# Covariance attention on one Trainium2 core: half of one unit's store leaves as 68 and 60 partitions in place of 85, 32 and 11

## The chip, the core and the metric

The kernel runs on one core of a Trainium2 chip. The time is that of the device, in microseconds (us). Of the kernel before there are three runs: 129.61, 129.66 and 130.15, median 129.66. A profiled execution comes beside them, 129.72, and all durations in this document are from its trace. The core has compute engines (PE for matmuls, DVE, ACT and POOL for the rest), a queue engine (SP) that issues most of the transfers here, and 16 DMA engines that carry them.

## The reference

Q, K and V are `[8, 12, 512, 64]` in float32. For each of the 96 heads the columns of Q and K are normalised over the 512 positions, a 64 x 64 matrix is made from them, and its softmax multiplies V:

```
Q_norm = Q / (norm(Q, axis=-2) + 1e-10)
K_norm = K / (norm(K, axis=-2) + 1e-10)
attn = softmax(einsum('bhnd,bhne->bhde', Q_norm, K_norm), axis=-1)
out = einsum('bhnd,bhde->bhne', V, attn)
```

There is much to move for little to compute: 37.75 MB are read and 12.58 MB written.

## The kernel before, in words

The 96 heads are worked on in S = 12 units of 8 heads, numbered 0 to 11. Each unit has 1 MB of Q, 1 MB of K, 1 MB of V and 1 MB of output. Two units make a pair that shares its tiles of V (there are W = 6 pairs).

For one unit, Q and K are loaded (`load_qk`, L219 and L221), cast to bf16 (`cast_qk`), squared (`square`) and multiplied to Gram matrices (`grams`, L260). The sums of squares give the norms (`sums`, `fold`, `norms`, `powers`). The scaled matrix goes through the softmax (`scale_k`, `logits`, `scales_q`, `exps`, `normalise`). V is loaded (`load_v`, L225), cast and transposed, and the product with it is made in four parts (`outs`, L338), each of which `ocopy` (L205 on ACT, L207 on DVE) copies into the unit's output tile `so`: 128 partitions, each with two halves (r = 0 and 1) of 1024 numbers, that is 4096 bytes a half. The pool of `so` has 6 buffers.

The order of all instructions on every engine comes from a planner (`Order`): it is given each piece of work with an estimated cost, what must come before it and a rank, and it lists the pieces in the order in which it would begin them. The store of a unit is one piece for it, whose cost doesn't depend on how the store is cut.

All loads but the two pieces of the first K are issued from the SP queue, and so are all stores, in the planner's order. `store(s, i)` (L227 to L236) issues one transfer for a unit (L234), 1024 KB, with one exception. Unit S - SPLIT = 9, the third from the end, is stored half by half, and each half is cut along its partitions as the table `CUTS` says (L228 to L232): half 0 as partitions 0 to 85, 85 to 117 and 117 to 128, and half 1 whole. Behind these four transfers come those of unit 10 and unit 11, and then the kernel waits until all stores have landed; the profile shows that wait under L512.

In DRAM the 128 partitions of one half are 128 rows of 4096 bytes that lie one behind the other, so each partition of a half is one packet of 4096 bytes for one DMA engine.

Of the kernel before, what the change touches and what calls it, by code (L numbers as in the profile page):

```python
# [56 lines left out]
 'V_PACE': 0.7666,  # L57
 'ST_LAG': 6.0835,
 'SPLIT': 3,
 'CUTS': (((0, 85), (85, 117), (117, 128)), ((0, 128),))}  # L60

D = 64
T = 32
# [453 lines left out]
```

## Time and profile before

| what | value |
|---|---|
| median of three runs | 129.66 us (129.61 to 130.15) |
| profiled execution, its own time | 129.72 us |
| its span, first to last instruction | 127.6 us |
| busy share of PE, DVE, ACT, POOL | 63%, 63%, 67%, 37% |
| DMA packets, bytes | 11601, 50.59 MB |
| share of the 16 DMA engines' span for SP's queue (q1) | 94.2% |
| instruction blocks of 16 KB (q8) | 14, 0.6% |
| last compute instruction ends | 114.9 us |
| issue of the four transfers of unit 9 | from 109.94 us on |
| issue of unit 10 and unit 11 | 112.69 and 114.89 us |

The span is cut into 40 equal slices in the page, about 3.2 us each; a digit is the busy share of a slice in tenths. In the list of DMA issues, KB is the size of one transfer, and the last number is the time from its issue to its landing. A landing is known from the completion marks: each DMA engine that has a part of a transfer sends one mark behind its last packet. A wait table names the waiting engine and line, what it waited for, the total, the number of times and the longest wait.

### The profile page before, as it was taken

Reading aid. Unit: us, or ns where it says so; the run is one execution under the profiler, and the core shown is the slowest. Engines: PE = TensorE matmul, PEld = TensorE weight load, DVE = VectorE, ACT = ScalarE, POOL = GpSimd, SP = SyncE. Lnnn points to the kernel's source line nnn. Section 1 sums busy time; section 2 is a strip of 40 time slices with the busy share of each in tenths; the row PEclk is TensorE's granted clock in tenths of the full one; section 3 lists DMA queues with packets and bytes.
Section 4 is the critical chain, followed back from the end, with each engine's and each line's share of the span. In section 5 each row is a group of like instructions: output and inputs, shape, how many; then the busy total and the mean of one; then the engine's idle time right before and its main releaser. Section 6 shows DMA issues by size and latency. Waiting matters only on the chain.

```text
span 127.6 us, 4062 instructions
## 1 busy us (share of the span) xinstructions
PE 80.8 (63%) x1800; PEld 54.0 (42%) x1800; DVE 80.4 (63%) x140; ACT 85.1 (67%) x116; POOL 47.0 (37%) x40
## 2 busy tenths in 40 slices
PE   0009459883797687676469897946999699950000
PEld 0006146560674365354336655532577267630000
DVE  2223344899836988889886699985699976600000
ACT  4076658794698826998798988839479757880000
POOL 3250665460545196054518805442516400000000
PEclk9999999999559999999976999995599967998555
DMA  4999999999999999999999999999999999999950
GB/s 117 412 419 437 421 414 437 408 420 416 429 420 429 419 420 408 421 415 428 407 434 415 416 419 420 428 414 416 430 419 416 414 417 414 415 416 406 408 234 15
DMA packets 11601, 50.59 MB, mean 396 GB/s; under 512 B 832, under 2 KB 832, under 8 KB 10048
## 3 DMA queue, kind: packets, MB, share of 16 engines
q1 hardware_dynamic: 11296, 49.29, 94.2%
q10 hardware_dynamic: 288, 1.05, 2.1%
q8 instruction: 14, 0.23, 0.6%
q14 instruction: 3, 0.02, 0.0%
HBM read 37.75 MB, written 12.58 MB: 394 GB/s over the span
## 4 chain that ended last, share of the span: by engine, by line
DMA 53%; PE 13%; DVE 12%; ACT 7%; SPq 4%; issue 2%
DMA qk<-in_Q_dram 36%; DMA v<-in_V_dram 17%; ACT so L205 4%; PE po L338 3%; SPq L225 3%; PE gram L289 3%; PE vps L323 3%; DVE ab L310 2%; PE l L266 2%; DVE vt L207 2%; PE gram L260 1%; DVE s L271 1%; ACT sq L251 1%; DVE sq L253 1%; ACT vb L205 1%
## 5 line engine op out<-in xcount | busy, mean ns | idle before, releaser
L209 POOL TENSOR_SCALAR kb<-qk 128x2048 bf16<-128x2048 f32 (+1 forms) x13 | 23.7, 1820 | 37.8 <-DMA qk<-in_K_dram 30.0
L251 ACT ACTIVATE sq<-qb 128x2048 bf16<-128x2048 bf16 (+1 forms) x13 | 23.1, 1778 | 8.2 <-DVE qb L207 8.2
L205 ACT COPY so<-po 128x512 f32<-128x512 f32 x47 | 25.6, 584 | 4.1 <-PE po L338 2.6
L209 POOL TENSOR_SCALAR vb<-v 128x1024 bf16<-128x1024 f32 x15 | 20.3, 1372 | 13.5 <-DMA v<-in_V_dram 9.8
L338 PE MATMUL po<-ab,vt 128*32 128x128 bf16 x768 | 20.6, 237 | 5.2 <-DVE ab L310 2.5
L260 PE MATMUL gram<-qb,kb 32*128 32x128 bf16 x768 | 15.3, 238 | 12.7 <-POOL kb L209 10.1
L323 PE MATMUL vps<-ident,vb 128*128 128x128 f32 x96 | 17.2, 304 | 4.9 <-POOL vb L209 2.7
L207 DVE CAST qb<-qk 128x2048 bf16<-128x2048 f32 (+1 forms) x12 | 13.6, 1137 | 10.3 <-DMA qk<-in_Q_dram 9.5
L266 PE MATMUL l<-sq,hm 128*32 128x512 bf16 x96 | 18.5, 446 | 2.1 <-ACT sq L251 1.5
L260 PEld LDWEIGHTS <-kb 32*128 32x128 bf16 x768 | 13.1, 104 | 14.8 <-POOL kb L209 11.4
L338 PEld LDWEIGHTS <-vt 128*32 128x32 bf16 x768 | 14.4, 103 | 11.2 <-issue 6.5
L207 DVE COPY vt<-vps 128x1024 bf16<-128x1024 bf16 (+1 forms) x25 | 16.5, 665 | 3.0 <-PE vps L323 2.7
L251 ACT ACTIVATE sq<-kb 128x2048 bf16<-128x2048 bf16 (+1 forms) x10 | 17.4, 1737 | 0.6 <-POOL kb L209 0.6
L205 ACT CAST vb<-v 128x1024 bf16<-128x1024 f32 x9 | 12.0, 1338 | 6.8 <-DMA v<-in_V_dram 6.8
L323 PEld LDWEIGHTS vps<-ident,vb 128*128 128x128 f32 x96 | 11.1, 151 | 8.7 <-POOL vb L209 3.3
L271 DVE TENSOR_REDUCE s<-l 64x128 f32<-64x512 f32 x12 | 8.1, 678 | 7.9 <-PE l L266 7.9
L289 PE MATMUL gram<-ident,kqs 128*128 128x128 f32 x48 | 9.7, 335 | 4.0 <-DVE kqs L285 3.7
L295 DVE TENSOR_TENSOR ls<-gram,r 64x256 f32<-64x256 f32 x24 | 10.1, 420 | 2.7 <-PE gram L289 2.3
L310 DVE TENSOR_TENSOR ab<-ex,rb 128x512 bf16<-128x512 f32 x12 | 10.4, 867 | 0.4
L285 DVE TENSOR_TENSOR kqs<-gram,r 128x512 f32<-128x512 f32 x12 | 8.3, 688 | 3.4 <-ACT r L281 2.9
L289 PEld LDWEIGHTS gram<-ident,kqs 128*128 128x128 f32 x48 | 6.2, 166 | 8.1 <-DVE kqs L285 7.3
L266 PEld LDWEIGHTS <-hm 128*32 128x32 bf16 x96 | 5.5, 104 | 9.4 <-issue 7.5
(25 smaller groups left out, 41.3 us busy)
## 6 DMA issues: line engine op xcount, KB each, us to landing
v<-in_V_dram SPq DMA_DIRECT2D x12, 1024.0 KB, 19.5
qk<-in_Q_dram SPq DMA_DIRECT2D x11, 1024.0 KB, 19.7
qk<-in_K_dram SPq DMA_DIRECT2D x11, 1024.0 KB, 19.7
out_dram<-so SPq DMA_DIRECT2D x11, 1024.0 KB, 15.3
qk<-in_K_dram ACTq DMA_DIRECT2D x2, 512.0 KB, 7.2
qk<-in_Q_dram SPq DMA_DIRECT2D x2, 512.0 KB, 5.8
out_dram<-so SPq DMA_DIRECT2D x1, 512.0 KB, 9.8
out_dram<-so SPq DMA_DIRECT2D x1, 340.0 KB
```

The lines of the kernel that those rows point to most:

```text
L205: nc.scalar.copy(o, i)
L207: nc.vector.tensor_copy(o, i)
L209: nc.gpsimd.tensor_scalar(out=o, in0=i, scalar1=1.0, scalar2=0.0, op0=ALU.mult, op1=ALU.add)
L251: nc.scalar.activation(o, i, AF.Square)
L260: nc.tensor.matmul(gram[s][:, h, 0], k, q, start=(t == 0), stop=(t == TT - 1))
L266: nc.tensor.matmul(st[s][32 * x:32 * (x + 1)].rearrange("p t d -> p (t d)"), hm, sq[s][:, x, t:t + 4].rearrange("p t r d -> p (t r d)"), s ...
L271: nc.vector.tensor_reduce(out=s2[s], in_=st[s].rearrange("p t d -> p d t"), axis=mybir.AxisListType.X, op=ALU.add)
L289: nc.tensor.transpose(gram[s][:, h, 1], kqs[s][:, h], ident)
L295: nc.vector.tensor_tensor(out=ls[s][half], in0=gram[s][half, :, 1, half], in1=r12[s][half, :HU, None].to_broadcast([D, HU, D]), op=ALU.mult)
L310: nc.vector.tensor_tensor(out=ab[s], in0=ex[s][:, :, None, :].to_broadcast([128, HU, 2, D]), in1=rb[:, :, :, None].to_broadcast([128, HU, ...
L323: nc.tensor.transpose(ps[:, n], vb[w][:, j].rearrange("p r d c -> p (r d c)").bitcast(F32), ident)
L338: nc.tensor.matmul(po[s, x][32 * h:32 * (h + 1), j].rearrange("p r d -> p (r d)"), v, ab[s][:, h].rearrange("p r d -> p (r d)"), start=Tru ...
```

## The change

One line of the table of parameters is changed:

```diff
  'ST_LAG': 6.0835,
  'SPLIT': 3,
- 'CUTS': (((0, 85), (85, 117), (117, 128)), ((0, 128),))}
+ 'CUTS': (((0, 68), (68, 128)), ((0, 128),))}
```

Half 0 of unit 9 leaves in two transfers, of 68 partitions (272 KB) and of 60 (240 KB), in place of three of 85 (340 KB), 32 (128 KB) and 11 (44 KB). The bytes, where they come from and where they go are the same, and so are half 1, all other stores, the loads, the compute instructions and the order that the planner gives them. There is one DMA instruction less on the SP queue.

## The prediction

> **What bounds the kernel now.** I read the page first, then the waits of the SP queue, then the DMA queues and the busy time over the last microseconds, and last the single DMA packets that the trace keeps (start, duration, size and queue of each; not the DMA engine).
>
> The page:
>
> ```profile
> span 127.6 us, 4062 instructions
> ...
> DMA  4999999999999999999999999999999999999950
> GB/s 117 412 419 437 421 414 437 408 420 416 429 420 429 419 420 408 421 415 428 407 434 415 416 419 420 428 414 416 430 419 416 414 417 414 415 416 406 408 234 15
> ...
> out_dram<-so SPq DMA_DIRECT2D x1, 512.0 KB, 9.8
> out_dram<-so SPq DMA_DIRECT2D x1, 340.0 KB
> ```
>
> The DMA engines are at 9 in every slice from the second to the last but two; no compute engine is over 67% of the span. The last two lines are of unit 9. The 340 KB are its 85 partitions; they have no time of landing, because the page gives one only where 16 completion marks came, one from each DMA engine. The semaphore records show six for it, five of them late (117.15 to 119.95): 85 partitions went out on 5 engines, 17 each. The 11 partitions have twelve marks, 11 of them late, so 11 engines with one each; the 32 have sixteen, so two each. In each case the count is the largest divisor up to 16. By that, 68 makes 4 engines of 17, and 60 makes 15 of 4.
>
> The waits of the SP queue near the end:
>
> ```profile
> SPq L512 <- DMA out_dram<-so: 11.3, 2, 8.9
> ```
>
> Compute is over at 114.9 us. SP then waits for the stores, 8.9 us for one of them: the end is the landing of unit 11. The stretches at the end, of which the last two columns count (DMA share, GB/s):
>
> ```profile
> 123.70:124.30 0.60, 0.00 (x0) 0.00 (x0) 0.00 (x0) 0.00 (x0) 0.00 (x0) 0.50 0.17 68
> 124.30:124.80 0.50, 0.00 (x0) 0.00 (x0) 0.00 (x0) 0.00 (x0) 0.00 (x0) 0.50 0.12 49
> 124.80:126.10 1.30, 0.00 (x0) 0.00 (x0) 0.00 (x0) 0.00 (x0) 0.00 (x0) 0.50 0.06 25
> 126.20:127.60 1.40, 0.00 (x0) 0.00 (x0) 0.00 (x0) 0.00 (x0) 0.00 (x0) 0.50 0.00 0
> ```
>
> 0.06 is one engine of sixteen, and 25 GB/s is a sixteenth of some 415. So from 124.8 on **one DMA engine** works alone. The kernel ends when the slowest of 16 engines does, not when the sum of the bytes is moved.
>
> **The sixteen tracks.** A 4096-byte packet takes 0.159 us and the next on its engine starts 0.155 after it. A full 1 MB transfer gives each engine 16 packets and a 4-byte mark, and the marks of one engine come 2.49 us apart, true to some 0.01. So the packets can be sorted into 16 tracks. Those that lie behind have had instruction blocks to carry: 16 KB blocks at 21.9, 29.9 and so on to 116.7 each put one track back by about 1.41. Marks behind unit 8 (us), then the last mark:
>
> - With 17 packets of the 85 (20 in all, then 8, 16 and 16): L1 and L2, 114.04 to 123.39; A, 114.87 to 124.22; B, 114.58 to 124.63; X, 116.70 to 126.17.
> - With 2 and 1 (3 in all): six tracks, 113.96 to 116.77; last marks 120.67 to 123.48.
> - With 2 alone: five tracks, 114.53 to 117.10; last marks 121.07 to 123.65.
>
> X is the engine of the last window, 1.54 behind B. It was no later than others until 95 us. From the second store on its packets took 0.166 to 0.29, and it lost 0.1 to 0.5 per unit; then at 116.1 a block of 8192 bytes (0.31) fell on it, and 17 packets came on top.
>
> **The change, track by track.** It moves the same 512 KB. SP issues two transfers in place of three; the issues of line 232 have a median of 0.35, so the three behind (half 1, units 10 and 11) may leave about 0.4 earlier. That is worth nothing: unit 11 was issued at 114.89 and its first packet starts after 118.17 on every track. If a track did run dry, the earlier issue would help. No wait is added, nothing is computed, and no buffer is freed that anyone waits for, as `so` has 6 buffers and no unit after 11 comes to take that of unit 9. So only the packets for each engine count:
>
> - Four engines: 17 + 4 = 21 in place of 20, and one mark of 0.006 less: +0.155 - 0.006 = +0.149.
> - The fifth: 4 in place of 20, two marks less: -16 x 0.155 - 0.012 = -2.50.
> - The next six: 4 in place of 3: +0.149. The next four: 4 in place of 2: +0.31. The last one: none in place of 2: -0.32.
>
> **Which of the five is the fifth?** This decides the case. That the four are among the five follows from nesting: each of the five also carries a mark of the 11. By count X is the fifth in 1 case of 5; the first packets say more. When the queue is empty at the start, at 1.76 to 2.15 us, the tracks differ, in fours. Four have a long second packet (0.29 to 0.51). Four have a long fifth (0.34 to 0.36) and a third of 0.16 to 0.17. Four have a long third (0.35 to 0.42) and 0.16 after it. The rest have another long packet in sixth place (0.20 to 0.37). Followed to the end, the first four are A, B, L1 and L2. The second four are X and three of the six. The third four are the other three of the six and one of the last five; the last four are the remaining four of those. If engines 0 to 3, 4 to 7, 8 to 11 and 12 to 15 behave alike in fours, the cuts at 5 and at 11 fall as seen, and X is the first of the second four: engine 4, the one that loses its 17. I take that.
>
> The Trainium skill, page "DMA: Bandwidth & Descriptors", section "Why a DMA increments its semaphore by 16 and not by 1", states the divisor and that such a transfer takes the lowest-numbered engines, which no run here shows directly. Its section "Latency and other measured facts" says that engines 7 and 15 are usually the slow ones. The trace speaks against that: the last track carries 17 packets of the 85 and so is one of five, not one of the later. By it, engine 7 would end the kernel and gain a packet: 129.87.
>
> **The sum.** X ends at 126.17 - 2.50 = 123.68. B becomes the last: 124.63 + 0.15 = 124.78; A 124.37, the latest of the others 123.65 + 0.31 = 123.96. A mark lands 0.33 later for B's (124.96) and 0.40 for X's (126.57). So the landing moves from 126.57 to 124.78 + 0.33 = 125.11, by 1.46. The rest stays: 127.6 - 126.57 = 1.03 to the end of the span, and 129.72 - 127.6 = 2.12 around it. 129.72 - 1.46 = 128.26. The profiled run is 0.06 above the median of 129.66, so I predict **128.2**.
>
> Two terms are unknown. B lost 0.70 between 116.9 and 118.4, in packets of 0.345, 0.526, 0.285 and 0.184, and the trace names no cause. If that is gone, B ends at 124.08 and A at 124.37 decides: 127.85, and 127.7 with some tenths of scatter. If it comes back, B holds; I take this, since the instruction blocks also come at fixed points. And X's slow spell, over at 116.9, may go on through its 44 packets: 2.75 units x 0.44 = 1.2, so 124.9, just past B: 128.4. Half such a spell on B, over its 61 packets (61 / 16 x 0.44 / 2 = 0.84), would make 129.1.
>
> **Rivals.**
>
> 1. X is one of the four, not the fifth. For it: the count alone gives 4 in 5. Against it: the pattern of fours, all of which fit. X would get one packet more: 126.17 + 0.15, so 129.87. No measurable change.
> 2. The slow spell is a matter of timing between tracks and passes to A or B once the loads shift. For it: X was in step with its neighbours to 0.02 us before it fell back. Against it: no other track had it in 30 us. B, with 61 packets at 0.44 per 16, would end at 124.78 + 1.68 = 126.46, 0.29 past X now: 130.0. No measurable change, though X is relieved.
> 3. Slower: the 68 go to two engines of 34 in place of four of 17. Then 17 packets more, 2.64, fall on the two first. It decides once A or B is one of them: B would end at 124.78 + 2.64 = 127.42, 1.25 past X now, so 131.0. Against it are the five and the eleven engines seen for 85 and 11; for it only that no 68 is in this trace. That the change fails to do what it says is this case too.
>
> **Chances.** The forecast 0.84, rival 1 0.09, rival 2 0.04, rival 3 0.03. So faster by over 0.5% (the bound of what a measurement of this kernel can tell from no change) 0.84, within it 0.13, slower 0.03. Range: 127.7 (B free of its delay) to 129.1 (half a slow spell on B); this leaves out the three rivals, 0.16.
>
> **What would show it.** Right: the 272 KB transfer has five marks and the 240 KB sixteen, of which one may come at once; the landing of unit 11 near 125.1; the stretch with one engine alone shorter, with B or A as its last. Wrong: a last mark near 126.3 that still belongs to X (rival 1), a new track with packets over 0.17 after 117 (rival 2), or three marks for the 68 (rival 3). All of it fails if the end of the span is no longer tied to the landing of unit 11.

## The result, and the profile after

The changed kernel takes 128.11 us, the median of four runs (127.95 to 128.12); the kernel before 129.68 beside it (129.61 to 130.15, the earlier runs among them). The ratio is 0.987, with a 95% interval of 0.985 to 0.989. Forecast were 128.2 and a range of 127.7 to 129.1. The profiled execution took 128.12, with a span of 126.0: 1.6 less than before, where the sum had 1.46.

One DMA of the SP queue is gone from the engines' lists of instructions, and the DMA engines carry 13 marks less; all else is as it was. The three transfers of unit 9 in the changed kernel's list of DMA issues (size, then issue to landing):

```profile
out_dram<-so SPq DMA_DIRECT2D x1, 512.0 KB, 10.0
out_dram<-so SPq DMA_DIRECT2D x1, 272.0 KB
out_dram<-so SPq DMA_DIRECT2D x1, 240.0 KB, 9.1
```

The 272 KB (68 partitions) have no landing: the semaphore records show five marks, one at once (109.58) and four late (117.08 to 117.80), so four engines. The 240 KB (60 partitions) have one: sixteen marks, one at once (110.02) and fifteen late. That is the divisor rule that was read from 85, 32 and 11; it also gives the marks of all transfers in the next four runs.

The waits of the SP queue after 105 us and the page of the changed kernel:

```profile
SPq L512 <- DMA out_dram<-so: 9.7, 1, 9.7
```

```profile
span 126.0 us, 4061 instructions
...
DMA  3999999999999999999999999999999999999982
GB/s 107 416 420 428 432 411 423 421 419 414 430 415 428 416 427 412 419 414 427 414 436 415 416 419 412 442 399 421 433 416 416 411 420 411 419 412 423 406 359 85
```

The wait for the last landing is still what ends the kernel. But the last two slices of the DMA row now read 8 and 2, where before the last three read 9, 5 and 0: the same packets are carried by engines that stop closer together. The stretches at the end (the last two columns: DMA share and GB/s):

```profile
122.60:123.40 0.80, 0.00 (x0) 0.00 (x0) 0.00 (x0) 0.00 (x0) 0.00 (x0) 0.50 0.72 297
123.95:124.25 0.30, 0.00 (x0) 0.00 (x0) 0.00 (x0) 0.00 (x0) 0.00 (x0) 0.50 0.13 55
124.35:124.50 0.15, 0.00 (x0) 0.00 (x0) 0.00 (x0) 0.00 (x0) 0.00 (x0) 0.50 0.07 27
124.60:125.99 1.39, 0.00 (x0) 0.00 (x0) 0.00 (x0) 0.00 (x0) 0.00 (x0) 0.50 0.00 0
```

Eleven or twelve engines work until 123.4 (0.72 of 16), two until 124.3, one until 124.56. Before, one engine worked alone from 124.8 to 126.2. The tracks, rebuilt from the packets as in the prediction: X had its mark behind unit 8 at 116.76 (116.70 before), then 4 packets, and ended at 123.62. A ended at 124.30 and B, the last, at 124.56. The last mark landed at 124.89, and 1.10 later the span was over.

### The profile page after: what moved, and what is told of

The parts are those of the page before. It is cut to its first block, busy times and chain, and to the rows that moved or that the text cites. A ratio compares the mean times of both kernels' runs of the same rounds, so it can differ in the third digit from the quotient of the medians.

```text
span 126.0 us, 4061 instructions
## 1 busy us (share of the span) xinstructions
PE 81.7 (65%) x1800; PEld 54.2 (43%) x1800; DVE 79.4 (63%) x140; ACT 85.0 (67%) x116; POOL 46.5 (37%) x40
## 4 chain that ended last, share of the span: by engine, by line
DMA 54%; PE 15%; DVE 11%; ACT 6%; SPq 3%; issue 2%; ACTq 0%
DMA qk<-in_Q_dram 31%; DMA v<-in_V_dram 17%; DMA qk<-in_K_dram 6%; PE po L338 4%; ACT so L205 3%; PE l L266 3%; PE gram L260 3%; SPq L225 3%; DVE ab L310 2%; PE vps L323 2%; PE gram L289 2%; DVE s L271 1%; ACT sq L251 1%; DVE vt L207 1%; ACT vb L205 1%
## 5 line engine op out<-in xcount | busy, mean ns | idle before, releaser
L266 PE MATMUL l<-sq,hm 128*32 128x512 bf16 x96 | 19.5, 470 | 1.7 <-ACT sq L251 1.1
L310 DVE TENSOR_TENSOR ab<-ex,rb 128x512 bf16<-128x512 f32 x12 | 9.4, 781 | 0.4
```

The lines of the kernel that those rows point to most:

```text
L266: nc.tensor.matmul(st[s][32 * x:32 * (x + 1)].rearrange("p t d -> p (t d)"), hm, sq[s][:, x, t:t + 4].rearrange("p t r d -> p (t r d)"), s ...
L310: nc.vector.tensor_tensor(out=ab[s], in0=ex[s][:, :, None, :].to_broadcast([128, HU, 2, D]), in1=rb[:, :, :, None].to_broadcast([128, HU, ...
```

## The experiments

The theory is that of the prediction: the fifth engine was last, and the change takes 16 packets from it. Two rivals would give the same result. The gain could come from the transfer less on the SP queue (rival 1 of the experiments). Or an uneven cut could be a gain in itself, since it gives more to engines that are ahead (their rival 2). Four runs tell these apart; each changes the cuts of half 0 of unit 9 only, and its edit is shown against the changed kernel. The kernel before took 129.62 beside them.

**One transfer of 128.**

```diff
- 'CUTS': (((0, 68), (68, 128)), ((0, 128),))}
+ 'CUTS': (((0, 128),), ((0, 128),))}
```

> Half 0 of unit 9 leaves in one transfer of 128 partitions, 8 packets for each engine. Theory (the fifth engine's 17 packets were the cost, the 21 on the first four are no gain in themselves): the fifth engine ends at 116.76 + 48 packets x 0.155 + 0.02 = 124.23, the latest of the others, whose mark behind unit 8 is at 117.04, at 124.51; A and B end near 122.4. So the last mark is within 0.1 of that of the 68 and 60, 124.56, and the time is 128.1. Rival 1 (each transfer less on the SP queue is worth some 1.5 us): 126.6. Rival 2 (the uneven cut is what gains, by giving the engines that are ahead more): slower than 68 and 60 by a us or more, 129.1 or above.

Measured: 128.17 (128.03 to 128.29), ratio to before 0.988 (0.987 to 0.990). The last mark came at 124.69. The time is that of 68 and 60, though half 0 goes out evenly and with a transfer less; the rivals had 126.6, and 129.1 or more. Both fail. The stretches:

```profile
122.60:123.40 0.80, 0.00 (x0) 0.00 (x0) 0.00 (x0) 0.00 (x0) 0.00 (x0) 0.50 0.56 230
123.45:124.10 0.65, 0.00 (x0) 0.00 (x0) 0.00 (x0) 0.00 (x0) 0.00 (x0) 0.50 0.46 189
124.25:124.35 0.10, 0.00 (x0) 0.00 (x0) 0.00 (x0) 0.00 (x0) 0.00 (x0) 0.50 0.30 123
124.70:126.10 1.40, 0.00 (x0) 0.00 (x0) 0.00 (x0) 0.00 (x0) 0.00 (x0) 0.50 0.00 0
```

The end is made in another way here. Seven engines are still at work from 123.45 to 124.1 and five at 124.3, where the changed kernel has two up to 124.25. Six engines were behind at unit 8 already (its marks landed from 117.12 to 117.59 for them, and by 116.34 for the others). With one more they end together, from 124.21 to 124.69; the other nine are done by 123.42.

**Two transfers, with the fifth engine in the first.**

```diff
- 'CUTS': (((0, 68), (68, 128)), ((0, 128),))}
+ 'CUTS': (((0, 95), (95, 128)), ((0, 128),))}
```

> Two transfers as in the changed kernel, but of 95 and 33 partitions: 19 packets on each of the first five engines and then 3 on each of eleven. The fifth gets 22, two more than with 85, 32 and 11. Theory: its last mark goes from 126.17 to 126.17 + 2 x 0.155 - 0.006 = 126.48 and the time is 130.0. Rival 1 (the number of transfers): 128.1, as with 68 and 60.

Measured: 130.15 (130.07 to 130.32), ratio to before 1.0039 (1.0024 to 1.0054). There are as many transfers as in the changed kernel, and the time is above that of the kernel before. The wait of the SP queue for the last landing is the longest of all runs with the cuts of unit 9 alone changed:

```profile
SPq L512 <- DMA out_dram<-so: 11.9, 1, 11.9
```

The stretches:

```profile
123.90:124.20 0.30, 0.00 (x0) 0.00 (x0) 0.00 (x0) 0.00 (x0) 0.00 (x0) 0.50 0.20 82
124.60:126.60 2.00, 0.00 (x0) 0.00 (x0) 0.00 (x0) 0.00 (x0) 0.00 (x0) 0.50 0.06 27
126.80:128.20 1.40, 0.00 (x0) 0.00 (x0) 0.00 (x0) 0.00 (x0) 0.00 (x0) 0.50 0.00 0
```

One engine alone again, now for more than two microseconds. Its last mark is at 126.73, not 126.48. Followed back, it had 19 packets of the 95 and its mark behind unit 8 at 117.07, 0.37 later than in the kernel before. In that kernel it had lost another 0.1 right behind the mark, in a packet of 0.262, which it did not lose here. So the two packets cost what was forecast (0.3), and the rest of the shift of 0.56 was there before them.

**Three transfers, without the fifth in the first.**

```diff
- 'CUTS': (((0, 68), (68, 128)), ((0, 128),))}
+ 'CUTS': (((0, 68), (68, 116), (116, 128)), ((0, 128),))}
```

> Three transfers as in the kernel before, of 68, 48 and 12 partitions: 17 packets on four engines, 3 on each of sixteen, 1 on each of twelve. The first four get 21, the fifth 4, as in the changed kernel, and the last four 3. Theory: B and A end as with 68 and 60, one mark later (0.006): 128.1. Rival 1 (the number of transfers): 129.7.

Measured: 128.06 (127.89 to 128.63), ratio to before 0.988 (0.986 to 0.991), last mark at 124.42. With as many transfers as before, the whole gain is there. With the run above, this closes the question: 95 and 33 put their many packets on five engines and end late; 68, 48 and 12 put them on four and do not. What separates the two is the fifth engine. Followed back, B ends last here (124.42) and A just before it (124.38). The transfers of unit 9:

```profile
out_dram<-so SPq DMA_DIRECT2D x1, 512.0 KB, 9.4
out_dram<-so SPq DMA_DIRECT2D x1, 272.0 KB
out_dram<-so SPq DMA_DIRECT2D x1, 192.0 KB, 8.8
out_dram<-so SPq DMA_DIRECT2D x1, 48.0 KB
```

The stretches at the end:

```profile
123.90:124.30 0.40, 0.00 (x0) 0.00 (x0) 0.00 (x0) 0.00 (x0) 0.00 (x0) 0.50 0.15 61
124.45:125.70 1.25, 0.00 (x0) 0.00 (x0) 0.00 (x0) 0.00 (x0) 0.00 (x0) 0.50 0.00 0
```

The 272 KB and the 48 KB, on four and on twelve engines, have no landing, and the 192 KB on all sixteen have one. Two or three engines are left after 123.9 and none after 124.45.

**Two engines in place of four.**

```diff
- 'CUTS': (((0, 68), (68, 128)), ((0, 128),))}
+ 'CUTS': (((0, 34), (34, 114), (114, 128)), ((0, 128),))}
```

> Half 0 as 34, 80 and 14 partitions: 17 packets on two engines, 5 on each of sixteen, 1 on each of fourteen. The first two get 23, the next twelve 6, the last two 5. Theory: A and B are known to be among the first four, but not which. If the first two are L1 and L2, they end at 114.19 + 63 x 0.155 + 0.03 = 124.0, the latest of the others at 117.04 + 46 x 0.155 + 0.03 = 124.2, so the last mark is at 124.2 and the time 127.8. If A or B is one of the first two: 124.6 to 124.9 and 128.2 to 128.5.

Measured: 127.93 (127.87 to 128.10), ratio to before 0.987 (0.985 to 0.989), last mark at 124.39. Neither case has this time; it lies between the two. The marks of the 34 partitions come from two engines (landed at 117.50 and 117.55), and followed on, these two are the last, at 124.34 and 124.39. The last one has its mark behind unit 8 at 114.57 and fits B, which speaks for the second case; B then started from an earlier point (114.75 in the changed kernel) and lost nothing on the way. The run does not beat 68 and 60 by more than the measurement tells. The stretches, with eight engines up to 123.95 and between one and two at 124.2:

```profile
123.72:123.95 0.23, 0.00 (x0) 0.00 (x0) 0.00 (x0) 0.00 (x0) 0.00 (x0) 0.50 0.48 196
124.10:124.30 0.20, 0.00 (x0) 0.00 (x0) 0.00 (x0) 0.00 (x0) 0.00 (x0) 0.50 0.10 41
124.40:125.70 1.30, 0.00 (x0) 0.00 (x0) 0.00 (x0) 0.00 (x0) 0.00 (x0) 0.50 0.00 0
```

What made the fifth engine late before it got its 17 packets? Two more runs asked whether its slow spell goes with the engine or with the partitions that it carries. **Both are inconclusive.** In the first, the kernel before stores units 0 to 8 by halves of the partitions:

```diff
-            nc.sync.dma_start(out=Of[s // 2, s % 2], in_=so[s].rearrange("p r j d -> p r (j d)"))
+            for a, b in PAR["PARTS"](s):
+                nc.sync.dma_start(out=Of[s // 2, s % 2][a:b], in_=so[s][a:b].rearrange("p r j d -> p r (j d)"))
...
+ 'PARTS': lambda s: ((64, 128), (0, 64)) if s < 9 else ((0, 128),)}
```

> The kernel before, with its cuts of 85, 32 and 11, but the stores of units 0 to 8 leave as two transfers of 64 partitions each, the upper ones (64 to 128) first. Each engine still gets 16 packets per unit, now of other partitions (8 of the upper half, 8 of the lower), and one mark more. The question is what made the fifth engine late before it got its 17 packets: the slow spell from the second store on, with packets of 0.166 to 0.29. Theory a (the spell belongs to the engine): it comes again from about 94.5 us on one track of the five, and the time stays at 129.7. Theory b (the spell belongs to the partitions or the rows of DRAM that this engine had, 8 in a row): no track of the five has it, the fifth ends some 2.4 us earlier at 123.8, and the time is 128.1 to 128.3, set by A or B as with 68 and 60.

Measured: 131.61, with single runs from 130.2 to 136.5; ratio to before 1.011 (1.004 to 1.018), without the longest. The longest (136.53) is the one with the profile, so the trace does not tell what the others did. Neither theory had this time. The second run leaves the last 32 partitions of units 1 to 4 out of the output:

```diff
-            nc.sync.dma_start(out=Of[s // 2, s % 2], in_=so[s].rearrange("p r j d -> p r (j d)"))
+            n = 96 if s in (1, 2, 3, 4) else 128
+            nc.sync.dma_start(out=Of[s // 2, s % 2][:n], in_=so[s][:n].rearrange("p r j d -> p r (j d)"))
```

> The kernel before, but of units 1 to 4 only the first 96 partitions are stored (the last 32 rows of each half are left out of the output). Each engine then gets 6 packets per half of those units, and the fifth engine has partitions 24 to 29 in place of 32 to 39; from unit 5 on all is as before. Everything behind is 4 x 4 x 0.155 = 2.5 us earlier on the DMA engines. Theory a (the slow spell belongs to the engine): one of the five tracks loses 0.1 to 0.5 per unit in units 1 to 4 too. Theory b (it belongs to the partitions or rows): that track loses nothing until unit 5, and another one, of the six, loses time in units 1 to 4.

Measured: 129.83 in a single run, and 129.52 in a single run of the kernel before beside it. A megabyte less was moved and no time was gained. In the stretch in which units 1 to 4 leave, this kernel first and the kernel before second, the last column falls from 414 to 365 GB/s at the same DMA share:

```profile
97.00:107.00 10.00, 8.80 (x258) 5.85 (x261) 7.69 (x18) 7.99 (x15) 2.79 (x2) 1.00 1.02 365
```

```profile
97.00:107.00 10.00, 8.50 (x205) 5.60 (x207) 8.27 (x15) 6.98 (x14) 2.62 (x2) 0.83 1.02 414
```

From 97.3 on, packets of 0.17 to 0.45 and more stand on four or five tracks at a time, where the kernel before has them on one at most times. The same comes again from 113 to 119 us, when units 8 and 9 leave, which this kernel stores as the kernel before does (again this kernel first):

```profile
113.00:119.00 6.00, 0.62 (x16) 0.35 (x15) 0.00 (x0) 1.10 (x3) 0.00 (x0) 0.50 0.99 346
```

```profile
113.00:119.00 6.00, 0.77 (x43) 0.42 (x31) 0.00 (x0) 1.66 (x3) 0.00 (x0) 0.82 1.03 412
```

With that the spell of a single track can no longer be told, and its cause stays open.

## Why the prediction was right, point by point

**What ends the kernel.** Right: the landing of unit 11, and in it one engine. In the six kernels that differ in the cuts of unit 9 alone, the time of the profiled execution follows its last mark: 124.39 and 127.87, 124.42 and 127.89, 124.56 and 128.12, 124.69 and 128.23, 126.17 and 129.72, 126.73 and 130.32. The difference is 3.47 to 3.59.

**How many engines a transfer takes.** Right, by the marks of 68 and 60. That the 68 go to two engines (rival 3 of the prediction) is out.

**Which engine is last.** Right. The pattern of fours in the first packets made X the fifth. In the changed kernel X is a track with 4 packets, and the pair of runs with and without the fifth engine shows it without any pattern. Rival 1 of the prediction (X one of the four, 129.87) is out, and so is an engine outside the five as the last one.

**The sum.** X was forecast to end at 123.68 and did so at 123.62; A at 124.37 and 124.30; the latest of the others at 123.96 and 123.90. The last mark was forecast at 124.78 and came at 124.56. The mis-sized term is B's own delay: 0.70 was carried over from the trace before, and in the new trace B lost 0.31 between the mark of its 17 packets (117.39) and that of its 4 (118.33: 0.94, where 0.63 was due). B's mark behind unit 8 was 0.16 later, which took part of that back, and the way from the landing to the end of the span was 1.10 in place of 1.03. That the median came within 0.1 of the forecast is thus in part luck: two smaller errors ran against the larger one. What delays B stays open.

**The slow spell.** The assumption that it is over when the packets of unit 9 come held: X had no long packet after 117 in the changed kernel. Before that the spell came again, beginning between 94.5 and 95.6 us, in the runs that left the stores of units 0 to 8 as they were. Rival 2 of the prediction, that it passes to a loaded engine, did not happen: after 117 B had two long packets (0.221 and 0.380), the 0.31 of the sum, and no spell behind them.

**What the transfer less is worth.** Nothing, as said: one transfer less again (128 whole) and one more (68, 48 and 12) leave 128.17 and 128.06.

The gain is thus one of not loading the engine that is already last. It does not need the uneven balance of 68 and 60: sending half 0 whole does as well within the measurement. The extra packets on the first four engines fill time that these had, and then make two of them the last.

How much was left to gain can be worked out from the tracks. The mean of the sixteen last marks is 123.08 before and after, as the same packets are carried. If all engines stopped together, the last mark would come there (an estimate). Before it came 3.1 later, and the change took 1.6 of that; about 1.5 is still there.

## What to carry to other kernels

When a kernel ends on its stores, look for the stretch in which the DMA share is one sixteenth: that is one engine working alone. The most that balancing can give is the distance from the last engine's end to the mean end of all sixteen (3.1 us here). The number of partitions in a transfer decides how many engines share it, so before cutting a store to shift load, find out which engines are behind and whether the cut loads one of them. An even transfer of 128 partitions is the version to beat: here it was as good, within the measurement, as the best uneven one (128.17 and 127.93).

## What the runs showed of the hardware that was not expected

- The engines keep their place behind one another: marks of one track lie 2.49 us apart over tens of transfers. An instruction block of 16 KB, a packet of 0.93, put its engine back by about 1.41 for the rest of the run.
- While transfers of 96 partitions left (6 packets of each half for each engine), the rate was 365 in place of 414 GB/s and many packets were long. But it was also 346 in place of 412 GB/s later in the same run, with units stored as before. So the 6 packets alone do not explain it, and the cause stays open.
- The fifth engine had longer packets (0.166 to 0.29) while units 1 to 8 were stored. The other engines had such packets mainly behind instruction blocks. Whether it is the engine or its partitions stays open.
